# A planned decoder layer: small products joined into one unit, two gate projections recorded later, the planner's marks and prices changed

## The chip, the cores and the metric

The kernel runs on one core of a Trainium2 chip. The metric is the device time of one execution in microseconds (us). Names of engines: PE is TensorE (matmuls and transposes), PEld its weight loads, DVE is VectorE, ACT is ScalarE, POOL is GpSimd, SP is SyncE, which issues all transfers (DMAs) of this kernel in one queue.

## What is computed

One layer on 1024 rows of 1024 values, in float32. Cut to its core:

```python
h = rms_norm(x, attn_norm_w)
proj = h @ w_in                       # a_q a_k a_v a_z | b_q b_k b_v b_z | i_q i_k i_w
# A: short causal conv on q, k, v; silu; l2 norm; gated delta rule, 4 heads, chunks along the sequence
for each chunk: v_new = val - kcd @ state ; o = qd @ state + att @ v_new
                state = state * g_last + kd.T @ v_new
o_a = rms_norm(o, a_out_norm_w) * silu(a_z)
# B: indexer scores, the 256 best keys of every row, softmax attention over these
score = sum_h iw[h] * relu(iq[h] @ ik.T) ; keep = top_k(score, 256)
o_b = softmax(bq @ bk.T, where kept) @ bv * silu(b_z)
x = x + concat(o_a, o_b) @ w_out
out = x + (p @ w_ple) * sigmoid(rms_norm(x) @ w_gate + b_gate)
```

## The kernel before

Everything lies transposed, features on partitions. A float32 product is made of three matmuls on split operands (hi and lo parts, `mm3`): hi by hi, hi by lo, lo by hi. In the order of time the program does: the norm and the transposes of x; the projections, in jobs of 128 output columns with two halves of 512 rows each (`Piq`, `Pak`, `Paq`, `Pav`, `Paz`, `Pbq`, `Pbz`: 24 matmuls 128x512 a half); the indexer's scores (`lg`); the delta rule (function `gdn`), beside which VectorE and ScalarE search the top-k thresholds (`junk`, `junka`) and write masks (`eq`, `cum`); attention (`S` scores, `P` softmax, `pt` transposes, `pv` value products); the output product (`oA` to `oD`), the embedding product (`ple`) and the gate (`g`).

For each of the four heads h the delta rule first inverts small triangular matrices (`inverse`, `merge`): six tiles `w0`, `x2`, `wa`, `wb`, `wc`, `wd` of products with 32 or 64 rows, 8 to 32 of them a tile, each tile waiting for the one ahead by way of ScalarE or VectorE. The trace calls them w, x, wa, wb, wc and wd. Then comes the recurrence (`gdn_s2`): 8 chunks with three matmuls in a chain (tile `rec0c` to `rec3c`) with one VectorE instruction between two of them (`r`, `vnew`, `S`), and per half a read-out `po`, its norm on ScalarE and POOL (`sqo`, `rs`, `o`), four transposes `to`, a product `z` on VectorE and a store `mixd<-z`.

Nothing of this is issued as it is written. `Plan` records every instruction as a node of a graph (`add`), gives it a price (`price`: `occ`, how long it holds its engine, and `lat`, how long until others may use its result), and places all nodes by priority (`forward`, `backward`, some rounds); `issue` then emits them in that order, which is the order of every engine's queue. An engine takes its instructions strictly in this order. Work that is ready is thus used to fill the time in which a chain waits, but only where the planner has put it.

Pools of memory are opened and closed by nodes of their own, called marks. In the kernel before, each mark waits until the mark recorded ahead of it is done (`lastmark`), whatever memory the two are for. The pools of the projections lie on the left side: `hT` (the operand of all projections) and `fill` (their staging). After the last projection `tail_open` closes them and opens `x2` in their place: the embedding's operand (`praw`, then `pTh` and `pTl`), the residual `x` and the mix chunks. The pools of the delta rule and the top-k lie on the right side, in PSUM (`gdns`, `gdnr`) and in SBUF; when they have closed, attention opens its own there: `kvst` with `kst` (keys) and `vst`, `atta`, `attb`, `atts`.

`drive` records jobs of the stream (projections, `ple`, output) beside chains. A job named in `holds` is recorded only after the event beside it; `gdn` in that list is the end of the delta rule with its pools closed. The line before:

```python
self.holds = [..., ("av3", "s2_1"), ("mix0", "gdn"), ("oB0", "t3"), ("oD0", "tail")]
```

The stream's order ends with `bz0 bq2 az3 bq3 bz1 bz2 bz3`, then the opening of x2, six `ple` jobs, `mix0`, and the output jobs. bz0 to bz3 are the projections of the gate z_B; each half is followed by a tanh on ScalarE (`fth`), a product on VectorE (`fz`) and a store `zd<-fz`.

Of the kernel before, what the change touches and what calls it, by code (L numbers as in the profile page):

```python
# [10 lines left out]
BF16 = mybir.dt.bfloat16  # L11
# [76 lines left out]
class View:  # L88
# [27 lines left out]
    def real(self):  # L116
        r = self.t.get()
        for op in self.path:
            r = op(r)
        return r  # L120
# [68 lines left out]
class DramTile:  # L189
    dram = True  # L190
    pool = None
# [29 lines left out]

class Op:
    __slots__ = ("i", "eng", "fn", "args", "kw", "pre", "post", "occ", "lat", "port", "bytes", "pool", "tile", "prio",
                 "start", "end", "n", "ready")

    def __init__(self, i, eng):
        self.i, self.eng, self.pre, self.post = i, eng, {}, []
        self.occ = self.lat = self.bytes = 0
        self.port, self.pool, self.tile = False, None, None


# [8 lines left out]
class Plan:  # L240
# [2 lines left out]

    def __init__(self, tc):
        self.tc, self.nc, self.ops = tc, tc.nc, []
        self.held, self.lastmark, self.pin = {}, None, True
        for e in self.ENG:
            setattr(self, e, Queue(self, e))

# [22 lines left out]
    def mark(self, pool, opens, deps):  # L272
        op = self.new("mark")
        op.pool = (pool, opens)
        for o in deps:
            self.edge(o, op, 2)
        if self.lastmark is not None:
            self.edge(self.lastmark, op, 2)
        self.lastmark = op
        return op  # L280

    def add(self, eng, fn, args, kw):
        for x in list(args) + list(kw.values()):
            if isinstance(x, View) and not x.t.dram and not x.t.born:
                self.birth(x.t)
        op = self.new(eng)
        op.fn, op.args, op.kw = fn, args, kw
        outs = [args[0]] + [kw[k] for k in ("accum_out",) if k in kw]
        ins = [x for x in list(args[1:]) + [v for k, v in kw.items() if k != "accum_out"] if isinstance(x, View)]
        outs = [x for x in outs if isinstance(x, View)]  # L290
        for x, write in [(x, False) for x in ins] + [(x, True) for x in outs]:
            t = x.t
            if not t.dram:
                self.edge(t.born, op, 2)
            p0, p1, m = x.region()
            keepers = []
            for e in t.log:
                o, w, a, b, mm = e
                hit = a < p1 and p0 < b and mm & m
                if hit and (w or write) and o is not op:  # L300
                    self.edge(o, op, 0 if t.dram and w and write else 2 if w else 1)
                    if write and p0 <= a and b <= p1 and not mm & ~m:
                        continue
                keepers.append(e)
            keepers.append((op, write, p0, p1, m))
            t.log = keepers
            if not t.ops or t.ops[-1] is not op:
                t.ops.append(op)
        if eng == "tensor":
            t = outs[0].t  # L310
# [18 lines left out]
    def price(self, op, outs, ins):  # L329
        n = max([x.free() for x in outs + ins], default=1)  # L330
        on = lambda x: x.t.pool is not None and x.t.pool.space is not None
        fn, kw = op.fn, op.kw
        acc = "accum_out" in kw
        if op.eng == "sync":
            o = next((x for x in outs + ins if not x.t.dram), None) or ins[0]
            op.occ, op.bytes = 120, int(np.prod(o.ix.shape)) * SIZE[o.dt]
            op.lat = 2000
        elif op.eng == "tensor":
            n, m, k = outs[0].free(), ins[0].free(), ins[0].ix.shape[0]
            op.lat = 165  # L340
            if fn == "transpose":
                op.occ = 109
            elif F32R in (ins[0].dt, ins[1].dt):
                op.occ = max(112, n / 2.4 + 13.5)
            else:
                op.occ = 14 if k <= 32 else 140 if k <= 64 else max(215, 4 * n / 2.4 + 8)
        elif op.eng == "scalar":
            op.occ = 40 + .92 * n + (90 if isinstance(kw.get("scale"), View) else 0) + (140 if acc else 0)
            op.lat = 100
        elif op.eng == "vector":  # L350
            two = len([x for x in ins if x.free() > 1]) > 1
            ps = any(on(x) for x in outs + ins)
            if n <= 8:
                op.occ = 80
            elif "scan" in fn:
                op.occ = 40 + 1.9 * n
            elif fn in ("tensor_copy", "memset", "transpose") or (fn == "tensor_scalar" and not ps and not acc):
                op.occ = 100 + .55 * n
            elif fn == "tensor_reduce":
                op.occ = 110 + .6 * n  # L360
            else:
                op.occ = 131 + .92 * n + (60 if acc and fn == "tensor_scalar" else 0)
            op.lat = 84
            op.port = two and not ps and n > 8
        else:
            two = fn == "tensor_tensor"
            op.occ = 150 + (2.15 if two else .95) * n
            if kw.get("op") == OP.pow:
                op.occ = 340 + 160 * n
            op.lat = 40  # L370
            op.port = two and n > 64
        if op.eng != "sync":
            op.lat += 100
# [29 lines left out]

    def gap(self, p, o, kind):

        same = p.eng == o.eng and p.eng != "sync"
        if kind == 0 or same and (kind == 1 or p.eng == "tensor"):
            return p.start
        return p.end

    def forward(self):
# [13 lines left out]
        n = len(ops)  # L425
        while n:
            s, e = min((max(free[e], 0 if avail[e] else pend[e][0][0]), e) for e in pend if avail[e] or pend[e])
            while pend[e] and pend[e][0][0] <= s:
                o = heapq.heappop(pend[e])[2]
                heapq.heappush(avail[e], (-o.prio, o.i, o))  # L430
            o = heapq.heappop(avail[e])[2]
            if o.port and port[other[e]] > s:
                alt = next((x for x in sorted(avail[e])[:6] if not x[2].port), None)
                if alt:
# [3 lines left out]
                    o = alt[2]  # L438
# [11 lines left out]
            if e == "sync":  # L450
                pipe = max(pipe, s + 1300) + o.bytes / 280
                o.end = pipe + 700
            else:
                o.end = s + o.occ + o.lat
            n -= 1
# [42 lines left out]
    def issue(self, order):  # L498
        first = {}
        for o in order:  # L500
            if o.tile:
                o.tile.left = set(o.tile.ops)
        real = lambda x: x.real() if isinstance(x, View) else x
        for o in order:
            if o.pool:
                p, opens = o.pool
                if opens:
                    p.cm = self.tc.tile_pool(**p.kw)
                    p.pool = p.cm.__enter__()
                else:  # L510
                    p.cm.__exit__(None, None, None)
                continue
            if o.tile:
                o.tile.get()
                continue
            f = getattr(getattr(self.nc, o.eng), o.fn)
            r = f(*[real(x) for x in o.args], **{k: real(v) for k, v in o.kw.items()})  # L517
            self.tc.keep_in_program_order(r)
            for x in list(o.args) + list(o.kw.values()):
                if isinstance(x, View) and not x.t.dram and not x.t.begun:  # L520
                    x.t.begun = True
                    key = x.t.pool, x.t.tag
                    if key in first and first[key].engine != r.ins.engine:
                        self.tc.add_manual_dep(r.ins, first[key].name, mybir.DependencyInfo(
                            mybir.DependencyClass.NoSync, mybir.DependencyReason.DATA), reason="turn")
                    first[key] = r.ins
            for x in list(o.args) + list(o.kw.values()):
                if isinstance(x, View) and not x.t.dram and self.spent(x.t, o):
                    x.t.tile = None

# [120 lines left out]
class Layer:  # L651
# [848 lines left out]
    def jobs(self):  # L1500
# [16 lines left out]
            else:  # L1517
                self.conv_job(st, nm, 4 * "qkv".index(nm[1]) + int(nm[2]))
        self.done = set()
        self.holds = [("aq2", "s2_0"), ("aq3", "s2_1"), ("av1", "tv0"), ("ak2", "tv1"), ("av2", "s2_0"), ("ak3", "tv2"), ("av3", "s2_1"), ("mix0", "gdn"), ("oB0", "t3"), ("oD0", "tail")]  # L1520

        def opened(w):
            self.tail_open()
# [489 lines left out]
```

## Time and profile before

| | |
|---|---|
| time, median of 3 runs (lowest to highest) | 889.71 us (889.05 to 891.18) |
| the profiled execution | 890.91 us |
| its span, first to last instruction | 889.1 us |
| TensorE busy | 855.1 us (96%) |
| VectorE, ScalarE, POOL busy | 607.5, 582.0, 476.6 us |
| granted TensorE clock, mean | 0.988 of full speed |

Busy time counts an engine as busy from an instruction's start to its end; matmuls overlap, so the pace of matmuls is read from the distance of their starts. In the rows below a line number (L517) is always that of the one place where the planner emits, so groups are told apart by tile names.

### The profile page before, as it was taken

The numbers are of one execution on the slowest core, as the hardware profiler recorded it, in microseconds if no ns is written. First come the engines' busy times: TensorE is split into PE (matmuls) and PEld (weight loads), VectorE is DVE, ScalarE is ACT, GpSimd is POOL, SyncE is SP. The second block draws the span as 40 slices with busy tenths as digits, with TensorE's granted clock in tenths as the row PEclk, the third lists the DMA queues.
The fourth block names the chain that finished last, engine by engine and source line by source line (L and its number), as shares of the span: only waits on it lengthen the run. The fifth ranks groups of instructions, "written<-read, shape, count | busy, mean of one in ns | idle before, by whom it ended". The sixth has DMA issues, their size and how long they took to land.

```text
span 889.1 us, 15490 instructions
## 1 busy us (share of the span) xinstructions
PE 855.1 (96%) x5231; PEld 709.1 (80%) x5231; DVE 607.5 (68%) x1394; ACT 582.0 (65%) x1289; POOL 476.6 (54%) x651
## 2 busy tenths in 40 slices
PE   8999999999999999999999998689999999999997
PEld 7988888888777787788788886458888888887885
DVE  5536364586788988999888475677687678655344
ACT  5645454455669898969899633688787577644432
POOL 2253122332456666557657545377576487657851
PEclk9999999999999999999999899799999999999999
DMA  7122111133113112311242113975344411236463
GB/s 265 73 97 72 36 60 36 60 90 92 40 57 103 60 45 93 106 44 61 84 138 81 51 58 103 337 215 155 122 149 144 142 59 49 94 120 214 129 196 113
DMA packets 79455, 94.23 MB, mean 106 GB/s; under 512 B 24176, under 2 KB 40592, under 8 KB 79248
## 3 DMA queue, kind: packets, MB, share of 16 engines
q1 hardware_dynamic: 79376, 93.25, 32.9%
q8 instruction: 41, 0.67, 0.3%
q14 instruction: 38, 0.31, 0.1%
HBM read 67.77 MB, written 25.45 MB: 105 GB/s over the span
## 4 chain that ended last, share of the span: by engine, by line
PE 79%; DVE 8%; ACT 5%; DMA 3%; issue 2%; POOL 2%; SPq 1%; DVEq 0%; POOLq 0%; ACTq 0%
PE g L517 10%; PE Piq L517 7%; PE lg L517 5%; PE Paq L517 4%; PE Pbq L517 4%; PE Pbz L517 4%; PE pv L517 4%; PE S L517 4%; PE Pak L517 4%; PE pt L517 3%; PE Pav L517 3%; PE Paz L517 3%; PE sm L517 2%; PE ple L517 2%; DVE acc L517 2%
## 5 line engine op out<-in xcount | busy, mean ns | idle before, releaser
L517 POOL TENSOR_TENSOR low<-raww,hiw 128x512 fp32r<-128x512 f32 x138 | 188.1, 1368 | 180.4 <-ACT hiw L517 129.7
L517 ACT ACTIVATE hiw<-raww 128x512 fp32r<-128x512 f32 x138 | 86.1, 628 | 60.5 <-PE g L517 14.3
L517 ACT ACTIVATE junka<-score,nt 128x1024 bf16<-128x1024 int16 (+1 forms) x96 | 109.9, 1145 | 4.5 <-DVE score L517 1.7
L517 PE MATMUL S<-kst,qT 128*128 128x384 f32 (+4 forms) x192 | 63.4, 376 | 12.1 <-DMA kst<-kd 9.5
L517 DVE TENSOR_SCALAR_CACHE_REDUCE junk<-score,cand 128x384 bf16<-128x384 f32 (+2 forms) x96 | 71.2, 741 | 1.7
L517 POOL TENSOR_SCALAR P<-P,rsum 128x128 f32<-128x128 f32 (+7 forms) x64 | 50.4, 796 | 31.3 <-DVE nm L517 11.9
L517 ACT ACTIVATE P<-P,nm,rq 128x128 f32<-128x128 f32 (+7 forms) x64 | 55.2, 864 | 17.1 <-DVE nm L517 15.4
L517 ACT ACTIVATE relu<-lg 128x512 f32<-128x512 f32 (+3 forms) x80 | 37.6, 523 | 40.8 <-PE lg L517 38.7
L517 DVE TENSOR_TENSOR pl<-pt,ph 128x512 fp32r<-128x512 f32 x72 | 48.1, 687 | 19.5 <-ACT ph L517 18.7
L517 DVE SCALAR_TENSOR_TENSOR score<-relu,sm,score 128x512 f32<-128x512 f32 (+5 forms) x42 | 41.3, 998 | 27.6 <-ACT relu L517 27.5
L517 POOL TENSOR_SCALAR nt<-acca,upa 128x1 f32<-128x1 f32 x96 | 34.6, 361 | 45.3 <-ACT junka L517 43.3
L517 PE MATMUL pt<-ident,P 128*128 128x128 f32 x288 | 51.9, 276 | 1.1 <-POOL P L517 0.6
L517 PEld LDWEIGHTS S<-kst,qT 128*128 128x128 f32 x192 | 35.5, 201 | 21.4 <-DVE qT L517 12.3
L517 ACT ACTIVATE ph<-pt 128x512 fp32r<-128x512 f32 x72 | 40.6, 593 | 17.5 <-PE pt L517 17.0
L517 PEld LDWEIGHTS pt<-ident,P 128*128 128x128 f32 x288 | 36.9, 141 | 13.7 <-POOL P L517 3.4
L517 PE MATMUL Piq<-hTlo,hiw 128*128 128x256 f32 (+1 forms) x128 | 41.0, 343 | 0.0
L517 PE MATMUL Piq<-hThi,hiw 128*128 128x256 f32 (+1 forms) x128 | 40.4, 345 | 0.1
L517 PE MATMUL Piq<-hThi,low 128*128 128x256 f32 (+1 forms) x128 | 39.7, 340 | 0.0
L517 DVE CUSTOM_DVE_ANT_0 P<-S,score 128x384 f32<-128x384 f32 (+3 forms) x48 | 28.5, 598 | 5.8 <-PE S L517 3.3
L517 DVE TENSOR_TENSOR gth<-g,rb 128x512 f32<-128x512 f32 x16 | 11.1, 691 | 29.4 <-PE g L517 24.0
L517 PE MATMUL pv<-ph,vst 128*128 128x512 f32 x72 | 29.7, 413 | 0.6 <-DVE ot L517 0.6
L517 PE MATMUL pv<-pl,vst 128*128 128x512 f32 x72 | 29.3, 407 | 0.0
(623 smaller groups left out, 2828.1 us busy)
## 6 DMA issues: line engine op xcount, KB each, us to landing
raww<-in_w_ct_dram SPq DMA_DIRECT2D x66, 256.0 KB
raww<-in_w_out_dram SPq DMA_DIRECT2D x32, 256.0 KB
raww<-in_w_gate_dram SPq DMA_DIRECT2D x32, 256.0 KB
xt<-in_x_dram SPq DMA_DIRECT2D x8, 512.0 KB
pled<-plt SPq DMA_DIRECT2D x16, 256.0 KB
pld<-pled SPq DMA_DIRECT2D x16, 256.0 KB
out_dram<-gth SPq DMA_DIRECT2D x16, 256.0 KB
scr<-gcd SPq DMA_DIRECT2D x8, 256.0 KB
```

The source lines that it names most:

```text
L517: r = f(*[real(x) for x in o.args], **{k: real(v) for k, v in o.kw.items()})
```

## The change

It has four parts.

- **Units.** A matmul whose weights have at most 64 rows is `small`. If it writes the same tile as the small matmul recorded just ahead of it, it becomes a further part of that node instead of a node of its own. The node's parts are emitted one after the other.
- **Marks.** A mark waits for the end of the last mark of its own kind (memory space and side) and only for the start of the last marks of other kinds; and in the planner's clock a mark starts when what it follows has started, and ends when what it must wait for has ended.
- **Hold.** `("bz2", "gdn")` is added: the last two gate projections, and with them the opening of x2 and the six `ple` jobs, are recorded after the delta rule's pools have closed.
- **Prices.** Numbers in `price` change for small products, VectorE and POOL.

```diff
+        key = pool.space is not None, pool.kw["side"]
+        for k, m in self.marks.items():
+            self.edge(m, op, 2 if k == key else 0)
+        self.marks[key] = op
...
+        small = eng == "tensor" and args[1].ix.shape[0] <= 64
+        op = self.ops[-1] if self.ops else None
+        joined = small and op is not None and op.small and op.parts[0][1][0].t is args[0].t
+        if not joined:
+            op = self.new(eng)
+            op.small = small
+        op.parts.append((fn, args, kw))
...
-                op.occ = 14 if k <= 32 else 140 if k <= 64 else max(215, 4 * n / 2.4 + 8)
+                op.occ = max(215, 4 * n / 2.4 + 8)
+                if op.small:
+                    op.occ = 250 + len(op.parts) * (12 if k <= 32 else 60)
...
-                op.occ = 40 + 1.9 * n
+                op.occ = 40 + 2.3 * n
...
+        if o.eng == "mark":
+            return p.start
...
+            elif e == "mark":
+                o.end = max([s] + [p.end for p, k in o.pre.items() if k == 2])
...
+            for fn, args, kw in o.parts:
+                r = getattr(getattr(self.nc, o.eng), fn)(*[real(x) for x in args], **{k: real(v) for k, v in kw.items()})
...
-        self.holds = [..., ("mix0", "gdn"), ("oB0", "t3"), ("oD0", "tail")]
+        self.holds = [..., ("mix0", "gdn"), ("bz2", "gdn"), ("oB0", "t3"), ("oD0", "tail")]
```

What this moves, at three places. First PE where the delta rule ends and attention begins, before (`to` are the last transposes of the delta rule, `Pbz` the projections of z_B, `S` the first scores):

```order
L517 MATMUL Pbz_1_6227<-hThi,hiw 128x512
L517 MATMUL Pbz_1_6227<-hTlo,hiw 128x512
L517 MATMUL to<-ident,o 128x128 x4
L517 MATMUL Pbz_1_6227<-hThi,low 128x512
L517 MATMUL to<-ident,o 128x128 x4
L517 MATMUL S_0_6457<-kst,qT 128x256 x2
L517 MATMUL S_1_6458<-kst,qT 128x256 x2
```

and in the changed kernel the same place, the last transposes and the first of what follows them:

```order
L534 MATMUL Pbz_0_6270<-hTlo,hiw 128x512
L534 MATMUL Pbz_1_6115<-hThi,hiw 128x512
L534 MATMUL to<-ident,o 128x128 x4
L534 MATMUL Pbz_0_6270<-hThi,low 128x512
L534 MATMUL Pbz_1_6115<-hTlo,hiw 128x512
L534 MATMUL Pbz_0_6270<-hThi,hiw 128x512
L534 MATMUL Pbz_1_6115<-hThi,low 128x512
```

Before, nothing stands between the last transposes and the first scores; now 43 matmuls of the projections of z_B do, and five more among the first scores. Second SP's queue of transfers there, before (`kst` the keys, `Qt` the queries, `praw` the embedding's operand, `x` the residual):

```order
L517 DMA mixd<-z 128x512 x2
L517 DMA zd<-fz 128x512
L517 DMA raww<-in_w_ple_dram 128x512
L517 DMA Qt<-qd 128x4x128
L517 DMA kst<-kd 128x4x128 x2
L517 DMA Qt<-qd 128x4x128
L517 DMA vst<-vd 128x2048
L517 DMA praw_6475<-in_pT_dram 128x512
L517 DMA praw_6486<-in_pT_dram 128x512
L517 DMA kst<-kd 128x4x128
```

and now:

```order
L534 DMA mixd<-z 128x512
L534 DMA zd<-fz 128x512
L534 DMA Qt<-qd 128x4x128
L534 DMA kst<-kd 128x4x128 x2
L534 DMA Qt<-qd 128x4x128
L534 DMA vst<-vd 128x2048
L534 DMA kst<-kd 128x4x128 x4
L534 DMA zd<-fz 128x512
L534 DMA kst<-kd 128x4x128 x2
L534 DMA raww<-in_w_out_dram 128x512 x2
L534 DMA Qt<-qd 128x4x128 x2
L534 DMA zd<-fz 128x512 x2
```

The eight loads of keys now stand together ahead of everything of x2; `praw` and the residual follow behind the last two `zd` stores and a load of `zt`. Third PE in the small products of head 3, before (`tv` are transposes of that head, `rec2c` is the recurrence of head 2):

```order
L517 MATMUL rec2c_5758<-r,U 128x128
L517 MATMUL x_5803<-U_5134,W_748 32x16 x6
L517 MATMUL tv<-ident,acc_743 128x128
L517 MATMUL x_5803<-U_5134,W_748 32x16 x10
L517 MATMUL tv<-ident,acc_743 128x128
L517 MATMUL x_5803<-U_5134,W_748 32x16 x10
L517 MATMUL tv<-ident,acc_743 128x128
L517 MATMUL x_5803<-U_5134,W_748 32x16 x6
```

and now:

```order
L534 MATMUL po_4947<-S,yaq_3560 128x128
L534 MATMUL po_4947<-vnew,att 128x128
L534 MATMUL x_5632<-U_4892,W_743 32x16 x32
L534 MATMUL rec2c_5571<-vnew,kh 128x128
L534 MATMUL fss<-sel,fsq 128x2
```

The 32 products of one tile stand in one run; over the whole program the small products stood in 34 runs and stand in 24, one for each of six tiles of four heads.

## Rows read from the trace of the kernel before

**Rows 1.** The page's first part: busy time of the engines.

```profile
PE 855.1 (96%) x5231; PEld 709.1 (80%) x5231; DVE 607.5 (68%) x1394; ACT 582.0 (65%) x1289; POOL 476.6 (54%) x651
```

**Rows 2.** Stretches: length, then each engine's busy time (x instructions), granted clock, DMA.

```profile
260.00:500.00 240.00, 235.23 (x1881) 192.27 (x1879) 204.62 (x545) 210.60 (x506) 155.90 (x331) 1.00 0.27 78
...
540.00:560.00 20.00, 12.03 (x66) 9.79 (x64) 6.82 (x12) 5.78 (x15) 6.90 (x10) 0.95 0.49 159
560.00:580.00 20.00, 15.74 (x67) 11.01 (x68) 15.41 (x76) 16.79 (x47) 9.28 (x18) 0.80 1.10 345
580.00:600.00 20.00, 17.23 (x78) 11.60 (x76) 16.18 (x46) 17.57 (x39) 15.21 (x16) 1.00 0.66 209
...
600.00:880.00 280.00, 278.16 (x1360) 227.55 (x1361) 177.91 (x405) 173.22 (x316) 185.23 (x152) 1.00 0.40 131
```

**Rows 3.** Waits of PE: who was waited for, total us, times, longest.

```profile
PE S L517 <- DMA kst<-kd: 9.5, 1, 9.5
```

**Rows 4.** Chain that ended last, around the wait: start, us, what.

```profile
553.87 1.26 POOL low L517
...
556.65 5.36 DMA kst<-kd
...
562.15 0.78 PE S L517 x2
```

**Rows 5.** PE's timeline: two projections in a row, last transposes, first scores.

```profile
549.76 0.39 PE L517 MATMUL Pbz<-hThi,hiw 128*128 128x512 f32 x1
549.99 0.39 PE L517 MATMUL Pbz<-hTlo,hiw 128*128 128x512 f32 x1
...
552.02 0.60 PE L517 MATMUL to<-ident,o 128*128 128x128 f32 x4
562.15 3.69 PE L517 MATMUL S<-kst,qT 128*128 128x256 f32 x12 [9.53 <-DMA kst<-kd]
```

**Rows 6.** SP's timeline: when each transfer was issued.

```profile
554.03 0.32 SPq L517 DMA_DIRECT2D zd<-fz  x1
555.16 0.33 SPq L517 DMA_DIRECT2D raww<-in_w_ple_dram  x1
555.54 0.45 SPq L517 DMA_DIRECT2D Qt<-qd  x1
556.03 1.25 SPq L517 DMA_DIRECT2D kst<-kd  x2
```

**Rows 7.** Stretches of 2 us, columns as in rows 2.

```profile
508.00:510.00 2.00, 2.00 (x15) 1.88 (x14) 0.69 (x1) 1.29 (x4) 1.72 (x3) 0.50 0.00 0
...
558.00:560.00 2.00, 0.00 (x0) 0.00 (x0) 0.00 (x0) 0.10 (x1) 0.00 (x0) 0.50 0.97 279
...
566.00:568.00 2.00, 1.98 (x9) 1.55 (x8) 1.91 (x13) 1.61 (x6) 1.28 (x3) 0.50 1.20 302
568.00:570.00 2.00, 1.40 (x9) 0.92 (x8) 1.81 (x10) 1.92 (x7) 1.72 (x4) 0.98 1.09 356
```

**Rows 8.** DVE's timeline: one mask instruction of the top-k, 512 keys.

```profile
535.19 1.30 DVE L517 SCALAR_TENSOR_TENSOR eq<-score,va,eq 128x512 bf16<-128x512 f32 x1
```

**Rows 9.** Chain around one run of small products, columns as in rows 4.

```profile
259.46 0.23 PE Pak L517
259.69 1.02 PE wa L517 x32
260.71 0.43 PE Paz L517
```

**Rows 10.** Instructions of tile praw: ns min/median/max, first to last start.

```profile
L517 SPq DMA_DIRECT2D praw<-in_pT_dram x4: 346/399/838, 559.0 to 581.1; - x4
L517 ACT ACTIVATE pTh<-praw x4: 616/620/632, 573.2 to 589.9; 128x512 fp32r<-128x512 f32 x4
```

**Rows 11.** Stretches with small products of heads 0 and 2, columns as in rows 2.

```profile
260.00:280.00 20.00, 19.55 (x180) 15.22 (x178) 15.03 (x39) 17.09 (x48) 11.66 (x34) 1.00 0.29 94
...
420.00:440.00 20.00, 19.60 (x290) 15.69 (x289) 17.11 (x44) 17.26 (x38) 12.90 (x30) 1.00 0.23 77
```

More of the change, by code (lines that the diff above doesn't have):

```diff
@@ L223 @@
     __slots__ = ("i", "eng", "fn", "args", "kw", "pre", "post", "occ", "lat", "port", "bytes", "pool", "tile", "prio",
-                 "start", "end", "n", "ready")
+                 "start", "end", "n", "ready", "small", "parts")
     def __init__(self, i, eng):
@@ L228, in __init__ @@
         self.occ = self.lat = self.bytes = 0
+        self.small, self.parts = False, []
         self.port, self.pool, self.tile = False, None, None
@@ L245, in __init__ @@
         self.tc, self.nc, self.ops = tc, tc.nc, []
-        self.held, self.lastmark, self.pin = {}, None, True
+        self.held, self.marks, self.pin = {}, {}, True
         for e in self.ENG:
@@ L276, in mark @@
             self.edge(o, op, 2)
-        if self.lastmark is not None:
-            self.edge(self.lastmark, op, 2)
-        self.lastmark = op
+        key = pool.space is not None, pool.kw["side"]
+        for k, m in self.marks.items():
+            self.edge(m, op, 2 if k == key else 0)
+        self.marks[key] = op
         return op
@@ L285, in add @@
                 self.birth(x.t)
-        op = self.new(eng)
+        small = eng == "tensor" and args[1].ix.shape[0] <= 64
[5 more added lines that the diff above has]
+        op.parts.append((fn, args, kw))
         op.fn, op.args, op.kw = fn, args, kw
@@ L353, in price @@
             if n <= 8:
-                op.occ = 80
+                op.occ = 100
             elif "scan" in fn:
-                op.occ = 40 + 1.9 * n
-            elif fn in ("tensor_copy", "memset", "transpose") or (fn == "tensor_scalar" and not ps and not acc):
+                op.occ = 40 + 2.3 * n
+            elif fn in ("tensor_copy", "memset", "transpose") or (
+                    fn == "tensor_scalar" and not ps and not acc and outs[0].dt != BF16):
                 op.occ = 100 + .55 * n
@@ L364, in price @@
             op.port = two and not ps and n > 8
+            op.occ += 60 + .1 * n if op.port else 0
         else:
             two = fn == "tensor_tensor"
-            op.occ = 150 + (2.15 if two else .95) * n
+            op.occ = (150 if two or n > 8 else 250) + (2.15 if two else .95) * n + (300 if fn == "affine_select" else 0)
             if kw.get("op") == OP.pow:
@@ L515, in issue @@
                 continue
[L516 to L519, printed above, removed]
+            used = []
+            for fn, args, kw in o.parts:
+                r = getattr(getattr(self.nc, o.eng), fn)(*[real(x) for x in args], **{k: real(v) for k, v in kw.items()})
+                self.tc.keep_in_program_order(r)
+                used += list(args) + list(kw.values())
+            for x in used:
                 if isinstance(x, View) and not x.t.dram and not x.t.begun:
@@ L526, in issue @@
                     first[key] = r.ins
-            for x in list(o.args) + list(o.kw.values()):
+            for x in used:
                 if isinstance(x, View) and not x.t.dram and self.spent(x.t, o):
@@ L1519, in jobs @@
         self.done = set()
-        self.holds = [("aq2", "s2_0"), ("aq3", "s2_1"), ("av1", "tv0"), ("ak2", "tv1"), ("av2", "s2_0"), ("ak3", "tv2"), ("av3", "s2_1"), ("mix0", "gdn"), ("oB0", "t3"), ("oD0", "tail")]
+        self.holds = [("aq2", "s2_0"), ("aq3", "s2_1"), ("av1", "tv0"), ("ak2", "tv1"), ("av2", "s2_0"), ("ak3", "tv2"), ("av3", "s2_1"), ("mix0", "gdn"), ("bz2", "gdn"), ("oB0", "t3"), ("oD0", "tail")]
         def opened(w):
```

## The prediction

> **What bounds the kernel now.** I read the page's busy times first. TensorE is busy 96% of the span, no other engine above 68% [rows 1], so a shorter time has to come from stretches in which TensorE stands still or runs slowly. The stretches say where these lie: in the 240 us of delta rule and top-k (260 to 500) it misses 4.8 us, in the 280 us of attention and output (600 to 880) 1.8 us, but in the 60 us between 540 and 600 it misses 8.0, 4.3 and 2.8 us [rows 2]. That is where the delta rule hands over to attention.
>
> The list of waits names the cause: the first scores S wait once, 9.5 us, for the keys kst [rows 3]. The chain shows the order: a POOL instruction (`low`, the split of a weight tile) at 553.87, then the load of kst, then S at 562.15 [rows 4]. On TensorE the last transposes `to` start at 552.02 and take 0.60; nothing follows until S [rows 5]. SP issues the keys at 556.03, behind a weight load that had to wait until that `low` had freed its buffer [rows 6]. So 3.4 us pass from the end of `to` to the issue (552.62 to 556.03) and 6.1 us from there to S.
>
> The wait costs more than itself. From about 558 the granted clock is at half, 1.2 instead of 2.4 GHz, and it stays there until about 568, six microseconds into the work that follows [rows 7]. There is a second such dip around 508.
>
> **The change part by part, worked out on the profiled execution (890.9 us, 1.2 us above the median of the runs).**
>
> *Hold and marks.* Both move the same thing and go together. In the order before, the pools of the delta rule could close only after the opening of x2, and so after the last gate projection; now they can close first, and 43 matmuls of bz2 and bz3 stand between the last `to` and the first S. Two such matmuls start 0.23 us apart [rows 5], so they fill 43 x 0.228 = 9.8 us. No matmul is added: the recurrence ends by that much less projection work earlier. When do the keys come? In SP's queue the store `zd` stands directly ahead of Qt and kst. Its `fz` stands on VectorE behind the last `z` and two mask instructions of the top-k; the mask one read here takes 1.30 us [rows 8], and short ones about 0.75 (estimate from the same row, taken as bound for an instruction not slowed by POOL: it has the same 512 elements as `z`). `z` 0.75, masks 1.5 to 2.6, `fz` 0.7: zd goes out 3.0 to 4.1 us after `to`, kst two issues of 0.5 us later [rows 6], and S could start 6.1 us after that: 9.6 to 11.2 us after `to`, against a cover of 9.8. What is left of the wait is 0 to 1.4 us, and I take 0.6. **Gain 8.9 us**, between 8.1 and 9.5.
>
> *The clock behind the wait.* Without the idle stretch nothing should take the clock down. From 562 to 568 TensorE was busy nearly throughout at half clock [rows 7]. At full clock that work would take half, so at most 2.9 us come back. But ScalarE is busy 16.8 and 17.6 of 20 us there [rows 2], which is the exponentials of the first blocks, so part of it only turns into waiting for ScalarE. **Gain 1.4 us**, between 0 and 2.9. The Trainium skill (TensorE: Matmul & The Clock Gate, "Part 1: The HAM clock gate") prices a throttled stretch by its length times the missing share of the clock; by it the term would be the full 2.9, and the row on ScalarE is why I take half.
>
> *Units.* The small products stand in 34 runs before and in 24 now. After a run the next 128x512 matmul holds the chain 0.43 us instead of 0.23 [rows 9], so ten runs fewer give back 10 x 0.20 = 2.0 us. If the long step is only the tail of the run's last product, which waits anyway, it is 0. **Gain 2.0 us**, between 0 and 2.0.
>
> *What comes late instead.* x2 now opens after bz3, so the embedding's operand `praw`, the residual and then the first `ple` come behind the last `fz`, which stands on VectorE among the softmax work of block 1. On PE the first `ple` now stands behind 41 matmuls of S, 24 transposes and 11 of pv, before behind 32, 14 and 2. That stretch was paced by ScalarE [rows 2], so attention's progress does not suffer, and fillers that are left out early are made up later (at the 76th S the same filler work has been issued in both orders, within 1 us). Bounds: 0 if `ple` finds its operand there, and the rival below if not. **Loss 1.0 us.**
>
> *Prices, and all else that moves.* The new numbers re-sort instructions from 40 us on. The recurrences keep about 1.1 to 2 us of other matmuls between two steps in both orders; I count no direction. Bound by what the delta rule's stretch misses, 4.8 us [rows 2], to gain, and as much to lose. **0.**
>
> Sum: -8.9 -1.4 -2.0 +1.0 = -11.3 us. 890.9 - 11.3 = 879.6 for a profiled execution, 1.2 less for a median: **878.5 us**.
>
> **The rivals.**
>
> *The wait comes back.* If the loads land later than the 6.1 us after issue, or VectorE is behind with its masks, each microsecond past the cover is lost. Against it: the key loads are no longer shared with `praw` and the residual. For it: `zd` and the masks ahead of them. With 5 us of waiting left, and half the clock term gone: 884.
>
> *`ple` stops TensorE.* This one ends on the other side. TensorE works in order, so if `pTl` is not there when the first `ple` is reached, S and pt behind it stand too. Before, `praw` was issued at 559.0 and `pTh` started at 573.2, 14.2 us later, while 345 GB/s moved [rows 2, 10]. Now `praw` goes out after the last `fz` and its store, some 16 us after the first S (estimate: 14 of 16 head passes of the first two blocks at the pace of the old stretch, about 1 us each). With 14.2 us again it is there 30 us after S, while PE reaches `ple` after about 20. The stall of 10 us eats the gain: about 889, no change. It decides at 34 us: from there on each microsecond makes the kernel slower than the bound of 0.3% (2.7 us, about what a measurement of this kernel can tell from no change), and with 40 us it stands at 898. Against it: the loads of keys and values are through by then, so `praw` should come sooner after its issue.
>
> *The clock falls at the units.* The dip around 508 came after the small products of head 3, which stood close together; it lasted 6.6 us at half clock, 3.3 us of lost work [rows 7]. If closed runs bring it at each of four heads, three dips more cost 9.9 us: 888. Against it: heads 0 and 2 have their small products nearly in closed runs already, with the clock at 1.00 [rows 11]. The same page of the Trainium skill (TensorE: Matmul & The Clock Gate, Part 1) lets the array's activity set the clock, and small products use little of the array; by that rule alone the dips would be likely, and the rows of heads 0 and 2 speak against it.
>
> *The change does nothing here.* Then the wait of rows 3 is still there. The order excludes that: work stands in it.
>
> **How the numbers follow.** The forecast (870 to 883) has 0.72, the wait that comes back 0.08 (about 884, still faster), `ple` that stops TensorE 0.14 (0.05 within the bound, 0.09 slower), the clock 0.04 (same), another loss in the re-sorted part above 14 us 0.02 (slower). So faster 0.80, same 0.09, slower 0.11. The best case takes every term at its end: -9.5 -2.9 -2.0 -4.8 = -19.2, or 870.5 as a median. The range goes from there to 887, which takes in the returned wait and a stall of `ple` up to 8 us.
>
> **What would show it.** In the profile after: the wait of S for kst is gone or below 1.5 us, and Pbz stands between the last `to` and S; the clock reads 1.00 from 540 to 580; the 128x512 matmul behind each small run still takes the longer step, in 24 places; TensorE's misses between the handover and 600 stay at 7 us or below. I would be wrong if S waits 4 us or more, if PE waits for pTl at the first `ple`, or if the granted clock falls near the small products.

## The result

Four runs of the changed kernel took 880.8 to 882.2 us, median 880.89, against 890.44 for the kernel before: a ratio of 0.9897 (95% interval 0.9879 to 0.9915), 9.6 us less. The profiled execution took 882.16 us with a span of 880.4, 8.7 less than before. The predicted time was 878.5, 11.2 less.

The page's first part and then the stretches of the changed kernel, with the columns of [rows 1] and [rows 2]:

```profile
PE 846.1 (96%) x5231; PEld 702.1 (80%) x5231; DVE 613.9 (70%) x1394; ACT 582.1 (66%) x1289; POOL 482.3 (55%) x651
```

```profile
260.00:500.00 240.00, 233.47 (x1903) 191.39 (x1902) 206.75 (x560) 211.61 (x516) 152.92 (x325) 1.00 0.27 77
...
540.00:560.00 20.00, 14.77 (x77) 10.66 (x75) 16.66 (x78) 17.01 (x48) 8.02 (x16) 0.99 0.95 289
560.00:580.00 20.00, 18.97 (x86) 14.58 (x85) 16.09 (x54) 18.28 (x42) 14.48 (x16) 0.92 0.80 263
580.00:600.00 20.00, 17.94 (x87) 13.37 (x87) 14.40 (x45) 18.68 (x40) 16.50 (x16) 1.00 0.62 197
...
500.00:600.00 100.00, 90.66 (x455) 70.93 (x454) 81.49 (x227) 71.77 (x172) 65.68 (x74) 0.98 0.60 190
...
780.00:882.00 102.00, 88.63 (x375) 70.60 (x373) 44.03 (x52) 36.05 (x59) 56.96 (x42) 0.94 0.47 152
```

Two more stretches of the kernel before, which answer to the last two:

```profile
500.00:600.00 100.00, 84.54 (x471) 66.57 (x468) 67.09 (x186) 57.49 (x145) 49.59 (x63) 0.91 0.53 169
...
780.00:890.00 110.00, 100.71 (x449) 80.69 (x447) 48.18 (x61) 43.11 (x71) 64.38 (x48) 0.98 0.47 156
```

Read them as an account. TensorE's span is its idle time, the busy time that a half clock adds, and the rest, its work at full clock. Idle time is a stretch's length less PE's busy time, and what the clock adds is busy time times the missing share of the clock, summed over stretches of 2 us.

- From 500 to 600 us idle time fell from 15.5 to 9.3 us, and what the clock adds from 6.1 to 1.6.
- From 780 us to the end of the span idle time rose from 8.4 to 11.8 us (100.4 - 88.6), and the clock, which added nothing there before, adds 3.0.
- From 260 to 500 us idle time rose from 4.8 to 6.5; elsewhere by 1.3 in all.
- Over the whole span idle time is the same, 34.0 and 34.4 us, the clock adds 4.6 in place of 6.1, and the work at full clock fell from 849.0 to 841.4 with the same 5231 matmuls. (The trace has two of them for each small product: the 32 products of a tile are 64 instructions there.)

The wait of S for its keys is gone. TensorE's timeline at the handover:

```profile
531.57 0.66 PE L534 MATMUL to<-ident,o 128*128 128x128 f32 x4
531.98 0.48 PE L534 MATMUL Pbz<-hThi,low 128*128 128x512 f32 x1
...
536.76 0.50 PE L534 MATMUL Pbz<-hThi,hiw 128*128 128x512 f32 x1 [0.42 <-DVE fz L534]
...
542.35 0.39 PE L534 MATMUL Pbz<-hThi,hiw 128*128 128x512 f32 x1
542.58 0.42 PE L534 MATMUL S<-kst,qT 128*128 128x256 f32 x2
```

and SP's queue there, whose last row shown is the operand of `ple`:

```profile
536.73 0.32 SPq L534 DMA_DIRECT2D zd<-fz  x1
537.10 0.43 SPq L534 DMA_DIRECT2D Qt<-qd  x1
537.63 1.25 SPq L534 DMA_DIRECT2D kst<-kd  x2
...
557.23 0.93 SPq L534 DMA_DIRECT2D praw<-in_pT_dram  x2
```

The keys go out 5.4 us after the end of `to` (532.23), and S runs 10.4 us after it with no wait: the 43 Pbz matmuls just reach. By the semaphore events of the trace the second load of keys landed at 542.4, 0.1 us before S.

### The profile page after: what moved, and what is told of

Read it like the earlier page. It is cut to its first block, busy times and chain, and to the rows that moved or that the text cites. A ratio compares the mean times of both kernels' runs of the same rounds, so it can differ in the third digit from the quotient of the medians.

```text
span 880.4 us, 15471 instructions
## 1 busy us (share of the span) xinstructions
PE 846.1 (96%) x5231; PEld 702.1 (80%) x5231; DVE 613.9 (70%) x1394; ACT 582.1 (66%) x1289; POOL 482.3 (55%) x651
## 5 line engine op out<-in xcount | busy, mean ns | idle before, releaser
L534 POOL TENSOR_SCALAR P<-P,rsum 128x128 f32<-128x128 f32 (+7 forms) x64 | 52.6, 829 | 40.2 <-DVE rsum L534 25.7
L534 POOL TENSOR_SCALAR nt<-acca,upa 128x1 f32<-128x1 f32 x96 | 37.1, 388 | 50.7 <-ACT junka L534 47.5
L534 PE MATMUL S<-kst,qT 128*128 128x384 f32 (+4 forms) x192 | 60.1, 361 | 1.7 <-DVE mx L534 1.7
L534 PE MATMUL Piq<-hThi,low 128*128 128x512 f32 (+1 forms) x128 | 40.2, 343 | 0.0
```

Of the source, the lines that this page charges most:

```text
L534: r = getattr(getattr(self.nc, o.eng), fn)(*[real(x) for x in args], **{k: real(v) for k, v in kw.items()})
```

## The experiments

Theory A was that the deferred projections (the hold) make the gain by covering the handover. In the table, idle time of TensorE in two stages and at the end, what the clock adds over the span, and the time from the first small product of each stretch to the start of the next other product, summed over the stretches ("small"). Each ratio is to runs of the kernel before taken beside that kernel (their medians lie between 890.4 and 891.1), so it is not the quotient of two rows. All but time and ratio are of one profiled execution; that one lies below the median of its kernel's runs by 3.8 us for the hold alone, 5.0 for the marks alone and 4.0 for "before, as recorded", elsewhere within 2.7 of it.

| kernel | median us | ratio to before (95%) | idle 260-500 | idle 500-600 | idle 780-end | clock | small |
|---|---|---|---|---|---|---|---|
| before | 890.4 | 1 | 4.8 | 15.5 | 8.4 | 6.1 | 25.8 |
| changed | 880.9 | 0.9897 (0.9879-0.9915) | 6.5 | 9.3 | 11.8 | 4.6 | 18.8 |
| hold alone | 891.0 | 1.0023 (0.9997-1.0048) | 11.1 | 6.7 | 8.4 | 3.2 | 25.8 |
| marks alone | 895.0 | 1.0034 (1.0011-1.0056) | 4.8 | 14.8 | 8.1 | 5.8 | 25.6 |
| prices alone | 896.9 | 1.0064 (1.0040-1.0089) | 4.9 | 16.3 | 8.4 | 13.2 | 26.4 |
| units alone | 891.8 | 1.0018 (1.0005-1.0031) | 11.0 | 16.4 | 8.4 | 4.7 | 19.4 |
| changed, no hold | 889.1 | 0.9984 (0.9960-1.0008) | 4.5 | 18.4 | 8.3 | 7.9 | 18.8 |
| changed, no marks | 878.4 | 0.9850 (0.9815-0.9885) | 5.6 | 9.2 | 11.7 | 4.6 | 18.8 |
| changed, no prices | 882.3 | 0.9909 (0.9884-0.9934) | 8.8 | 9.9 | 9.0 | 8.4 | 20.4 |
| changed, units cut | 888.2 | 0.9983 (0.9964-1.0003) | 5.7 | 8.5 | 11.6 | 6.0 | 21.4 |
| changed, units sorted | 896.9 | 1.0077 (1.0051-1.0103) | 4.5 | 8.1 | 10.8 | 9.6 | 34.1 |
| before, as recorded | 889.4 | 0.9973 (0.9952-0.9995) | 4.5 | 15.0 | 9.0 | 3.0 | 23.1 |
| changed, weights first | 879.2 | 0.9876 (0.9856-0.9896) | 5.9 | 7.7 | 12.2 | 3.1 | 18.9 |
| no prices, weights first | 891.6 | 1.0006 (0.9984-1.0027) | 9.3 | 9.1 | 15.2 | 7.2 | 18.9 |

### Each part alone

The hold alone, on the kernel before:

```diff
-        self.holds = [("aq2", "s2_0"), ("aq3", "s2_1"), ("av1", "tv0"), ("ak2", "tv1"), ("av2", "s2_0"), ("ak3", "tv2"), ("av3", "s2_1"), ("mix0", "gdn"), ("oB0", "t3"), ("oD0", "tail")]
+        self.holds = [("aq2", "s2_0"), ("aq3", "s2_1"), ("av1", "tv0"), ("ak2", "tv1"), ("av2", "s2_0"), ("ak3", "tv2"), ("av3", "s2_1"), ("mix0", "gdn"), ("bz2", "gdn"), ("oB0", "t3"), ("oD0", "tail")]
```

> The kernel before with the one new hold (the jobs of gate projections 2 and 3 wait for the recurrence's end) and nothing else of the change. Theory A (the gain is the handover wait, covered by deferred Pbz matmuls): 58 Pbz matmuls stand between the last `to` and the first S; 58 x 0.228 = 13.2 us is more than the wait of 9.5, so S waits under 1.5 us, TensorE is at full clock from 540 to 580, and the run takes about 881 us (878 to 884). Theory B (the gain comes from the new order that units and prices give elsewhere): the wait may go, but what is taken out of the stages before has to be paid there, and the run takes 887 to 892 us. By A the stretch at half clock at 506 to 513 us of the kernel before may stay, by B it has nothing to do with the hold and stays.

The wait went as theory A had it: no S waits for a DMA, idle time from 500 to 600 fell to 6.7 us. The time did not fall. From 260 to 500 us TensorE misses 11.1 us in place of 4.8. The largest of its waits there, with the columns of [rows 3]:

```profile
PE x L517 <- ACT xav L517: 2.4, 1, 2.4
PE tk L517 <- ACT sqj L517: 2.1, 2, 1.9
```

The time, 891.0, is theory B's. Neither theory has all of its signs: the clock was at half from 572 to 575, inside the stretch that A had at full clock, and the half clock at 506 to 513, which B had staying, is gone.

The marks alone:

```diff
-        if self.lastmark is not None:
-            self.edge(self.lastmark, op, 2)
-        self.lastmark = op
+        key = pool.space is not None, pool.kw["side"]
+        for k, m in self.marks.items():
+            self.edge(m, op, 2 if k == key else 0)
+        self.marks[key] = op
...
```

> The kernel before with only the marks of pools kept apart by memory and side. No Pbz matmul stands between the last `to` and the first S. Theory A: S waits 8 to 10 us as before, 890 us (887 to 893). Theory B (marks let pools open and loads go out earlier, so the wait shrinks without any cover): S waits under 5 us, 885 us or less.

S waits 9.6 us for kst: without deferred work the marks cover nothing. The time, 895.0, lies above the ranges of both theories; the trace is of the fastest of ten runs (890.0), so what slowed the others is not shown, beyond a lower mean clock (0.981 to 0.988 in them, 0.989 in this one).

The new prices alone, with the small products' old price and no units:

```diff
-                op.occ = 80
+                op.occ = 100
...
+            op.occ += 60 + .1 * n if op.port else 0
...
```

> The kernel before with only the new prices of VectorE and GpSimd (small products keep their old price and stay single). No cover at the handover. Theory A: S waits 8 to 10 us, 889 us (885 to 893). Theory B (the re-sorting by prices makes the gain of about 9 us ahead of and at the handover): 882 us or less with TensorE's work at 480 reached about 9 us sooner.

S waits 12.1 us for kst, and the clock adds 13.2 us: half clock from 502 to 513, 557 to 574, 581 to 584 and 820 to 823. The wait is longer than theory A's 8 to 10, and the time, 896.9, lies above the ranges of both theories. Nothing is gained ahead of the handover.

The units alone, with their price:

```diff
-        op = self.new(eng)
...
+        if not joined:
+            op = self.new(eng)
+            op.small = small
+        op.parts.append((fn, args, kw))
...
```

> The kernel before with only the units of small products and their price: 24 stretches of small products instead of 34, no cover at the handover. Theory A: S waits 8 to 10 us; 10 stretches fewer at 0.20 us give 888.4 us (886 to 891); whether the half clock at 506 to 513 us stays, A does not say. Theory B: the half clock behind the last head's small products goes (6 us) and the run takes 883 us or less, though S still waits 8 to 10 us.

S waits 10.0 us. The stretches take 19.4 us in place of 25.8, 6.4 less where the prediction had 2.0, and the half clock at 506 to 513 is gone, as theory B had it; but again the order has 11.0 us of idle time from 260 to 500, and the time, 891.8, lies above the ranges of both theories. Its largest waits there:

```profile
PE Paz L527 <- ACT yaq L527: 1.9, 1, 1.9
PE Pbq L527 <- DVE fz L527: 1.6, 1, 1.6
```

So no part alone gains. Theory A holds for the handover and falls for the time: each edit also makes the planner sort the recurrence anew, and two of the four orders lose 6 us there.

### The change without one part

The changed kernel without the hold (the diff of the hold alone, reversed):

> The changed kernel without the new hold: units, marks and prices stay. All Pbz matmuls run ahead of the recurrence's end; between the last `to` and the first S stand some `ple` products (6.8 us of them). Theory A (the hold is what covers the handover): `ple` needs `pTh`, which is made from loads that are themselves issued only behind the handover, so TensorE stands there as in the kernel before; idle and half-clock time from 500 to 600 us together are 19 to 23 us (10.9 in the changed kernel, 21.6 in the kernel before), and the run takes 889 to 893 us (ratio to the kernel before 0.999 to 1.003). Theory F (any filler does, the hold only chose which): 881 us (ratio 0.990).

Theory A in the wait and in the time; idle and half-clock time from 500 to 600 us together are 24.8, above its 19 to 23. Beside the other three parts the hold is worth 8.2 us (889.1 - 880.9), or 7.7 by the two ratios. TensorE's timeline shows the wait under another name:

```profile
540.82 0.66 PE L534 MATMUL to<-ident,o 128*128 128x128 f32 x4 [0.28 <-POOL o L534]
550.60 1.65 PE L534 MATMUL ple<-pTh,hiw 128*128 128x512 f32 x3 [9.12 <-ACT pTh L534]
```

Here `ple` stands first behind the handover, and its operand comes no sooner than the keys did. The filler has to be one whose data is already there.

Without the marks, units, hold and prices staying (the diff above, reversed):

> The changed kernel with one chain of marks for all pools as before: units, hold and prices stay. 61 Pbz matmuls stand between the last `to` and the first S. Theory A (the hold alone covers the handover, the marks have no time of their own): idle and half clock from 500 to 600 us stay at 8 to 12 us and the run takes 878 to 885 us (ratio 0.987 to 0.994). Theory G (with one chain the held gate projections keep the next stage's pools shut, so its loads are late and TensorE stands behind the cover): a wait of S or `ple` of 5 us or more, 887 us or more (ratio 0.997 or more).

Theory A: the hold does without the marks, and no S waits for its keys (the first waits 0.5 us for VectorE's `qT`). The intervals of this ratio and of the change overlap, so it isn't shown to be faster.

Without the new prices of VectorE and GpSimd (reversed too):

> The changed kernel with the old prices of VectorE and GpSimd: units, marks and the hold stay. 62 Pbz matmuls stand between the last `to` and the first S, and there are 24 stretches. Theory A (the hold covers the handover, worth 10 to 13 us with the clock; the units are worth 7; the prices only re-sort the rest): the handover wait is under 1.5 us and the run takes 877 to 885 us (ratio 0.985 to 0.994), lower than the changed kernel if the 6.4 us that it loses from 780 us on are the new prices' doing. Theory B (the prices carry the gain: without them the order has holes from 260 to 460 us as the hold alone had, 10.6 us of them): 887 to 892 us (ratio 0.997 to 1.002).

Theory A, at 882.3 us. Idle time from 780 us on is 9.0, not 11.8, but the recurrence has 8.8, and 13.7 us from 416 on run at half clock, so the time is not below the changed kernel's. The prices move losses about and have no gain that this run can tell.

### What the units are worth

No run leaves the units out of the change. Three runs price them in an order that otherwise stays as it is. First, each unit cut in two by a large product that stood just ahead of it:

```diff
...
+                h.parts, o.parts = o.parts[:len(o.parts) // 2], o.parts[len(o.parts) // 2:]
+                order.insert(i - 1, order.pop(j))
+                order.insert(i - 1, h)
...
```

> The changed kernel with 23 of its 24 units cut in two by one large product that stood just ahead of the unit: 47 stretches of small products in place of 24, nothing else moved. Theory C (a change between small and large products costs 0.20 to 0.30 us): 23 x 0.20 to 0.30 = 4.6 to 6.9 us, the run takes about 886.5 us (885 to 888.5; ratio to the kernel before 0.994 to 0.998). Theory D (all 7.0 us that the units saved were the 10 stretches fewer, 0.7 us each): 16 us more, 897 us (ratio 1.007).

7.3 us more than the change for 23 cuts, 0.32 each: theory C. In the two profiles the work at full clock rose by 7.2. TensorE's timeline of the cut kernel around one unit, and of the changed kernel around the same unit:

```profile
407.01 0.44 PE L534 MATMUL w<-T,NB 32*32 32x16 f32 x32
407.38 0.50 PE L534 MATMUL Paz<-hThi,hiw 128*128 128x512 f32 x1
407.81 0.44 PE L534 MATMUL w<-T,NB 32*32 32x16 f32 x32
408.18 0.50 PE L534 MATMUL Paz<-hTlo,hiw 128*128 128x512 f32 x1
408.52 0.40 PE L534 MATMUL Pav<-hThi,hiw 128*128 128x512 f32 x1
```

```profile
403.22 0.73 PE L534 MATMUL w<-T,NB 32*32 32x16 f32 x64
403.87 0.50 PE L534 MATMUL Paz<-hTlo,hiw 128*128 128x512 f32 x1
404.21 0.39 PE L534 MATMUL Pav<-hThi,hiw 128*128 128x512 f32 x1
404.44 0.40 PE L534 MATMUL Pav<-hThi,low 128*128 128x512 f32 x1
```

64 small and two large products take 1.51 us from first start to the next when cut, 1.22 in one piece: 0.29 for a change to small products and back. Of this only 0.09 lies between the first small product and the step behind it, which the column "small" counts; 0.20 lies in the steps of the large products. My 0.20 read only the step behind a stretch [rows 9].

Then the order inside a unit: sorted by the partitions written, in place of as recorded (`for c in range(8): for q in quad:`, which changes partitions at each product):

```diff
-            for fn, args, kw in o.parts:
+            for fn, args, kw in sorted(o.parts, key=lambda p: o.small and p[1][0].region()[0]):
```

> The changed kernel with one edit: within each unit the small products are sorted by the partitions that they write, in place of the order in which they were recorded, which changes partitions from product to product; 24 stretches as in the changed kernel, and no other instruction moves. The two traces so far show TensorE spending 18.8 us from the first product of each stretch to the large step behind it in the changed kernel and 25.8 in the kernel before, 7.0 less, where my prediction had 2.0 for the number of stretches alone. Theory C (products on the same partitions one after another can't overlap, and the units save by keeping the recorded order): `wa` x32 goes from 0.62 to about 1.0 us, `w` and `x` x64 from 0.65 to 1.5 or more, the sum of the stretches grows by 8 to 13 us and the run takes 889 to 894 us (ratio to the kernel before 0.998 to 1.004). Theory D (only the number of stretches counts): sum and time unchanged, 881 us (ratio 0.990).

16 us more, with 24 stretches as before: theory C, but above its ranges, also in the sum of the stretches, which grew by 15.3. The timeline:

```profile
407.99 1.89 PE L534 MATMUL w<-T,NB 32*32 32x16 f32 x64
409.81 0.50 PE L534 MATMUL Paz<-hTlo,hiw 128*128 128x512 f32 x1
```

The same 64 matmuls hold TensorE 1.82 us in place of 0.65. What the range had left out, too, is the clock, which adds 9.6 us here in place of 4.6: 6.6 of it near `w` and `x` of heads 2 and 3 (413 to 416 and 485 to 495 us), 3.0 in the output stage as in the changed kernel.

Last, the kernel before with nothing but the recorded order put back inside its 34 stretches:

```diff
...
+            for j, o in zip(run, sorted((order[j] for j in run), key=lambda o: o.i)):
+                order[j] = o
...
```

> The kernel before with one edit: in each of its 34 stretches the small products of one tile stand in the order in which they were recorded; no stretch is joined and nothing else moves. Theory C (order inside a stretch counts): `wa` and `wb` of the first heads fall from 1.00 to 1.37 us to about 0.63, the sum over the stretches falls by 2 to 3 us from 25.8, the time by as much, 888 us (ratio 0.996 to 0.999). Theory D (only the number of stretches counts): the sum stays at 25.8 (ratio 1.000).

The sum fell by 2.7 us, to 23.1, and the time by 0.27%. The `wa` that holds TensorE 1.02 us in [rows 9] now holds it 0.63:

```profile
258.90 0.69 PE L517 MATMUL wa<-T,NB 32*32 32x32 f32 x32
259.53 0.50 PE L517 MATMUL Paz<-hThi,hiw 128*128 128x512 f32 x1
```

In heads 2 and 3 more than the order changed. The 80 instructions of `wa` and `wb` stood in four stretches a head before, most of them 16 instructions of one tile, which the recorded order inside a stretch can't change. Such a stretch took 0.59 to 0.62 us, as long as 32 take in the changed kernel. `wa` of head 2 before and after:

```profile
430.09 0.66 PE L517 MATMUL wa<-T,NB 32*32 32x32 f32 x16 [0.40 <-DVE cand L517]
430.68 0.50 PE L517 MATMUL Pbz<-hThi,hiw 128*128 128x512 f32 x1
```

```profile
408.07 0.69 PE L534 MATMUL wa<-T,NB 32*32 32x32 f32 x32
408.70 0.50 PE L534 MATMUL Pav<-hTlo,hiw 128*128 128x512 f32 x1
```

Summed over both tiles and heads that is 5.7 us before and 2.5 after. The times fit stretches of one partition range each; the trace doesn't show the partitions.

### What the change lost in the output stage

The chain of the changed kernel there (start, us, what):

```profile
793.54 0.70 DVE x L534
...
794.26 0.64 ACT sqx L534
...
794.97 1.10 POOL ssum L534
...
796.32 0.92 POOL ssum L534
...
797.87 1.72 POOL low L534
...
799.64 4.63 PE oD__9352 L534 x10
```

The weights' split `low` stands in POOL's queue behind two `ssum` adds, which wait for the square of a tile just finished; on ScalarE the other split, `hiw`, stands behind the squares and h1 copies of such tiles. TensorE needs both and stands 4.0 us:

```profile
PE oD__9352 L534 <- ACT hiw L534: 2.8, 1, 2.8
PE oD__9352 L534 <- POOL low L534: 1.2, 1, 1.2
```

The clock is at half from about 799 to 805. The edit moves `hiw` and `low` ahead of such work in their queues; TensorE's order stays:

```diff
...
+        if name(o) in ("hiw", "low") and o.eng != "tensor":
+            j = i
+            while order[j - 1] not in o.pre and (order[j - 1].eng != o.eng or name(order[j - 1]) in ("ssum1", "sqx", "h1Ah", "h1Bh")):
+                j -= 1
+            order.insert(j, order.pop(i))
...
```

> The changed kernel with one edit from the output stage of the second half on: the splits of weights (`hiw` on ScalarE, `low` on GpSimd) are put ahead of the squares, h1 copies and `ssum` adds of finished output tiles that stand ahead of them in the two queues; TensorE's order is the same. Theory E (TensorE lost 4.0 us idle and 3.0 at half clock from 780 to 820 us because the weights queue behind these adds): `oD` waits for `low` and `hiw` under 1.5 us, clock 1.00, 4 to 6 us less than the changed kernel, 876 us (ratio 0.983 to 0.987). Rival (the loads of the weights come too late, whatever the queues do): the same time as the changed kernel, 881 us (ratio 0.990).

The waits for `hiw` and `low` at `oD` and the half clock there are gone. But POOL now has the splits first and the sums later, and TensorE waits 1.6 us for those; and it waits 2.2 for VectorE's `x`, which stands behind an instruction (`h1Al`) that needs ScalarE's h1 copy, now behind `hiw`. POOL's timeline, and TensorE's waits from 776 us on:

```profile
791.30 2.53 POOL L534 TENSOR_TENSOR low<-raww,hiw 128x512 fp32r<-128x512 f32 x2 [2.01 <-ACT hiw L534]
795.71 3.00 POOL L534 TENSOR_TENSOR ssum<-ssum,sqx 128x512 f32<-128x512 f32 x2 [1.89 <-ACT sqx L534]
```

```profile
PE oD__9381 L534 <- DVE x L534: 2.2, 1, 2.2
PE ssp L534 <- POOL ssum L534: 1.6, 1, 1.6
```

879.2 us: 1.7 less than the change, where 4 to 6 were expected, and the intervals overlap. Theory E named the queue rightly; but only the clock was won (3.0 us in this profile), and the idle time from 780 us on stayed, 12.2 for 11.8, with other names.

The same edit without the new prices:

> Units, marks and hold with the old prices, as in the run without the new prices, and the weights' splits put ahead of the finished tiles' work in the output stage. In the run without the new prices TensorE lost 0.1 us from 780 to 820 us, where the changed kernel lost 7.0. Theory E (the edit is worth what weights wait behind finished tiles): nothing to win from 780 to 820, at most the 2.3 us that gates waited for `hiw` behind 820; 880 to 882.5 us (ratio 0.988 to 0.991). Rival (what the edit gave the changed kernel was the order in general): 4 us less, 878 us (ratio 0.986).

Both theories failed: 9.4 us more than the same kernel without the edit, 8.6 by the two ratios. Its weights were not late from 780 to 820, so there the edit only put other work late. TensorE's waits:

```profile
PE ssp L532 <- POOL ssum L532: 4.1, 1, 4.1
PE g L532 <- ACT hiw L532: 3.2, 4, 1.6
```

Idle time from 780 us on went from 9.0 to 15.2, and the clock adds 2.4 from 831 on, where TensorE stands in the first of these waits.

## Why the prediction was right

The time came within 2.4 us, and the mechanism at the handover is the one forecast. That the sum came so close is in part luck, since its errors cancel. By the account above the profiled execution fell by 8.7 us: 6.1 of idle time from 500 to 600, 4.5 of clock there and 7.6 of work at full clock, less 9.5 lost elsewhere. The forecast had 7.9, 1.4, 2.0 and nothing.

- **Handover.** The mechanism is shown: the hold covers the wait, and the change without it stands 9.1 us for `ple` instead. I had -8.9 for the wait and +1.0 for later fillers, -7.9 together; idle time from 500 to 600 us fell by 6.1 (15.46 to 9.34). The cover itself reached, with 0.0 left to wait where I took 0.6, but narrowly, and by two sizes that cancel: the keys went out 5.4 us after `to`, where my terms give 4.0 to 5.1, and S had them 5.0 after that, not 6.1. (The sum of those terms begins at 10.1 us, not at 9.6.) The marks, which I put together with the hold, had no part in it: the change without them covers the wait as well. The later fillers are the mis-sized term: of the 15.5 us before, 9.5 were the wait, so 6.0 lay elsewhere in the stretch, and it is 9.3 now. I said that misses from the handover to 600 would stay at 7 us or below; from 540 they are 8.3. TensorE's longest waits from 500 to 620 are now for POOL's `P` (3.3 us in 7 waits) and VectorE's `mx` (1.7): softmax work with few fillers between, since `ple` starts only 23.8 us after S (11.7 before). The other runs bear this out: in the 60 us from the first S idle time is 6.8 to 8.6 us in all eight orders with the hold, and 4.6 to 5.3 in the five whose `ple` follows 12 to 16 us behind S. Covering the wait thus has a price of its own, about 3 us, where I had 1.0.
- **Clock behind the wait.** -1.4; behind the handover the clock now adds 1.6 in place of 2.9, so -1.3. But not as I had put it: the clock was not at 1.00 from 540 to 580. It was at half from about 560 to 563, after a stretch (544 to 560) in which TensorE was busy for two thirds of the time. And 3.2 us more came from the earlier dip, 506 to 513 [rows 7], which is absent in the changed profile. That it belongs to the change is not shown: the kernel before with the recorded order has the same large products there and shows no dip either, nor has any of the three parts hold, marks and units one there when it is alone.
- **Units.** -2.0, with 2.0 as the bound. Measured: the stretches take 7.0 us less. Of this 0.8 is one `wd` that ran at half clock before (1.90 us to the next step against 1.07); 1.9 is the order inside the stretches of heads 0 and 1, for which I had no term (2.7 less the same 0.8, by the kernel before as recorded); 3.2 is the joining of `wa` and `wb` in heads 2 and 3, and 1.0 that of other stretches, both read from the two traces and not run apart. The term's count of 10 was right and its price too low (0.29 to 0.32 for 0.20, so about 3), and some 2 of these 3 lie in the steps of large products, outside the 7.0. The longer step stands behind 18 of the 24 runs only, since behind the other six comes a smaller product.
- **Prices and all else.** 0 within 4.8 either way, from the recurrence. It cost 1.8 there, 1.3 elsewhere, and 6.4 from 780 us on (3.4 idle, 3.0 clock), for which I had no row: 9.5 in all, twice its bound. The bounds came from one stage only.
- **Rivals.** `ple` did not stop TensorE: `praw` went out 14.7 us after the first S (I had 16), `pTh` started 8.4 us later (not 14.2), and `ple` at 566.4 waited for nothing. The same rival came true in the change without the hold. The clock did not fall at the four heads' units; it did where the units were sorted.

What stays open is why the orders of the hold alone and of the units alone have 11 us of idle time from 260 to 500. The longest waits named are scattered, most of them for ScalarE, 1.1 to 2.4 us each. The hold's withheld fillers can't be the common cause, since the units alone withhold none. No run separates the orders further. Open, too, is what the change would take without its units.

## What to carry to other kernels

Cover a wait at a handover with work whose data is already there, and check the change both ways: by the part alone and by the whole without it. Here the part alone showed nothing (1.0023) and the whole without it showed 7.7 to 8.2 us: with the part alone the planner's new order had lost 6 us in another stage.

A sum over stages needs a term for each stage that the new order touches, also for one that missed nothing before. Small products belong together, with neighbours on different partitions. And an instruction moved ahead in a queue makes another late: the same edit took 1.7 us off one order, no more than the noise, and put about 9 on another.

## What the runs showed of the hardware

- 64 matmuls of 32x16 took 0.65 us with neighbours on different partitions and 1.82 with 16 in a row on the same ones. The Trainium skill (TensorEngine Tiling (Array Packing), "Key Properties") says that tiles of the array work independently and in parallel and that a change of tiling mode drains TensorE; the runs agree with the first by these two times, and put 0.29 to 0.32 us on a change from 128-row products to small ones and back, whatever it consists of.
- With the units sorted, the clock fell with no idle time ahead of it. Stretches of that kernel, columns as in [rows 2]:

```profile
408.00:410.00 2.00, 2.00 (x66) 1.97 (x66) 1.96 (x5) 0.48 (x2) 1.92 (x3) 1.00 0.00 0
410.00:412.00 2.00, 2.00 (x52) 1.59 (x53) 0.78 (x4) 1.84 (x4) 1.37 (x3) 1.00 0.09 19
412.00:414.00 2.00, 2.00 (x27) 1.68 (x25) 1.33 (x3) 0.00 (x0) 1.43 (x3) 0.77 0.79 248
414.00:416.00 2.00, 2.00 (x7) 1.71 (x6) 0.94 (x4) 1.80 (x4) 1.59 (x4) 0.50 0.01 3
```

  TensorE is fully busy, from 408 to 412 mostly with small products, and then the clock goes from 2.4 to 1.2 GHz. It fell again at 484.7, also with no idle time in the 8 us ahead of it. Two earlier heads with the same stretches show no fall.
- One program on one chip, the hold alone, took 887.0 to 896.3 us in ten runs. The two fastest had a mean granted clock of 0.990 and 0.994, the slowest the lowest, 0.979. A single run can hide 9 us.
